# One pool open over the up and down stages of a hybrid layer: down's first operands split during up's last block, up's first sums on GpSimd

## Chip, cores and metric

The kernel runs on one core of one Trainium2 chip. The metric is the device time of one execution in microseconds, the median of several. Engines are named as in the profile: PE (TensorE, matrix products), ACT (ScalarE), DVE (VectorE), POOL (GpSimd) and SP (SyncE, which here only issues transfers).

## What is computed

One layer of a streaming encoder trunk, for 2048 frames of a new stream and 64 frames of a running one: 2112 tokens of 1024 features.

```python
x = x + mix @ lp['w_out']
f = jax.nn.relu(_rms(x, lp['ln2']) @ lp['w_up'])
x = x + (f * f) @ lp['w_down']
```

`mix` comes from attention, a state-space branch and a short convolution, which the change doesn't touch. `w_up` is 1024 x 4096, `w_down` 4096 x 1024. All values are fp32. A product of two fp32 matrices is made of three products of halves: each operand is split into a high part (ACT copies it to the type fp32r) and a low part (DVE subtracts that copy from the value), and the products high-high, high-low and low-high are summed.

## The kernel before

The program runs in stages: in-projection, attention with the other branches between it, the out-projection with the norm (`phase3a`), which leaves the normed tokens in DRAM as `h_d` and the new x as `x2_d`, then `phase_up` and `phase_down`. Every stage opens its own pools of tiles on chip and closes them. A tile scheduler decides at build time in which order each engine's instructions stand, from the order of the code, what is ready and which buffers are free; an instruction that is given to `keep_in_program_order` is not moved. Engines, and the queues that issue transfers, work in the order of their queue: an instruction that waits holds all behind it.

**phase_up** (line 1538) computes relu(h @ w_up) squared with Strassen's scheme, seven products of half blocks in place of eight (`ORDER`). Tokens come in 3 blocks of 704, in two halves of 352; the columns of `w_up` in 16 groups of 256. One group in one block is a pair, numbered n = 0 to 47; each has 7 products of 12 matmuls 128x352 (line 1630). For each token block four sums of halves are made (`sums`, lines 1569 to 1575, 128x1408) and seven splits (`tokens`, 1582 on ACT, 1583 on DVE); for each pair four weight sums (`weights`, 1593 to 1596) and seven weight splits (1600, 1601, 128x512). The sums stand on DVE, but the weight sums of pair 0 on POOL. `pair` empties the product banks into the tile `sm` (copies on ACT at 1641, 1644, 1647, adds on DVE at 1650 to 1656), applies relu and square and stores `sm` to DRAM as `f_d` from SP's queue. `late_rows` finishes the norm of the last 128 prompt rows meanwhile, out of buffers of the first block (`late_x` reuses the slot of `hr0`).

**phase_down** (line 1696) multiplies `f_d` by `w_down` in 8 quarters of 4 weight rows `dw` (128x1024 each, split at 1712 and 1713) and 17 token tiles, 24 matmuls 128x512 for each tile (lines 106 to 108), summed into `acc` by DVE at 1764. Tokens are loaded again from `f_d` (`fr`, line 1718, SP) and split into `fh` and `fl` (1733, 1734). In the very first tile the loop runs over weight rows outside and halves inside. Before that loop the code stands as

```python
    for f in range(QF):
        load_w(f, nc.gpsimd)
    for f in range(2):
        split_w(f)
    load_f(*work[0])
    split_f(*work[0])
    for f in range(2, QF):
        split_w(f)
```

so that none of it can begin before the up stage's pools are free.

## Time and profile before

| | us |
|---|---|
| timed runs, median (lowest, highest) | 2822.74 (2819.06, 2823.24) |
| profiled execution, its time | 2809.31 |
| its span in the trace | 2807.6 |
| PE busy in the span | 2689.5 (96%) |
| DVE busy | 1692.3 (60%) |
| ACT busy | 1231.5 (44%) |
| POOL busy | 409.5 (15%) |

All rows are of the profiled execution, and their times count from the start of its span. A row of a timeline is one instruction, or several alike that follow each other: its start, its length (for several, from the first start to the last end), engine, line, operation, output<-input, count, and in brackets how long the engine stood idle before it and what ended that. A matmul's length is modelled and overlaps the next, so starts are compared there. A row of windows gives the busy time of each engine in a stretch and the granted clock of PE as a share of 2.4 GHz.

### The profile page before, as it was taken

To read this page: it belongs to the slowest core of one execution; us is meant where nothing else is said; L and a number is where in the kernel's file an instruction comes from. 1 tells how busy PE (TensorE), PEld (TensorE's weight loads), DVE (VectorE), ACT (ScalarE), POOL (GpSimd) and SP (SyncE) were. 2 spreads that over 40 slices of the span, in tenths; PEclk is the share of its full clock that TensorE was granted. 3 is DMA by queue.
4 is the path that set the end of the run, shared out by engine and by line. 5 is a ranking of instruction groups with operands and counts; after the bars stand their busy time and mean duration, and the time that the engine had idled before them with its cause. 6 is when DMAs were issued, how large, how long until landed. Compare 5 with 4: busy or idle time off the path is not lost.

```text
span 2807.6 us, 38902 instructions
## 1 busy us (share of the span) xinstructions
PE 2689.5 (96%) x14438; PEld 2335.1 (83%) x14438; DVE 1692.3 (60%) x3375; ACT 1231.5 (44%) x2383; POOL 409.5 (15%) x570
## 2 busy tenths in 40 slices
PE   7999998778899999999899999999989999999999
PEld 7999998755566776688789999999978888888887
DVE  7637468478465677577686686676644344434433
ACT  5424243156577678833265576675631111111110
POOL 2101105122662225422200000000000000000000
PEclk9999999889899999999999999999999999999999
DMA  7535545543634134375535353343354222212123
GB/s 217 187 109 184 161 111 170 109 98 92 102 97 111 44 93 116 102 217 163 183 132 176 130 180 128 127 167 127 127 188 128 64 79 80 78 47 78 49 75 120
DMA packets 365712, 347.12 MB, mean 124 GB/s; under 512 B 43342, under 2 KB 324254, under 8 KB 362542
## 3 DMA queue, kind: packets, MB, share of 16 engines
q1 hardware_dynamic: 362707, 335.53, 41.2%
q0 software_dynamic: 2816, 9.11, 1.0%
q8 instruction: 114, 1.87, 0.3%
q14 instruction: 75, 0.61, 0.1%
HBM read 237.05 MB, written 107.46 MB: 123 GB/s over the span
## 4 chain that ended last, share of the span: by engine, by line
PE 83%; DMA 5%; DVE 4%; ACT 3%; issue 2%; POOL 2%; SPq 1%; DVEq 0%; ACTq 0%; POOLq 0%
PE pa L1630 13%; PE pd L106 8%; PE pd L107 8%; PE pd L108 8%; PE pd L1630 6%; PE pb L1630 3%; PE pq L108 2%; PE pq L106 2%; PE pq L107 2%; PE mx L1146 2%; PE st L1237 2%; PE po L106 2%; PE st L1238 2%; PE po L1258 2%; PE po L107 2%
## 5 line engine op out<-in xcount | busy, mean ns | idle before, releaser
L1764 DVE TENSOR_TENSOR acc<-acc,pd 128x512 f32<-128x512 f32 x272 | 186.9, 687 | 420.8 <-PE pd L108 415.4
L106 PE MATMUL pd<-dw,fh 128*128 128x512 f32 x1024 | 399.4, 390 | 9.6 <-ACT dw L1712 9.6
L107 PE MATMUL pd<-dw,fh 128*128 128x512 f32 x1024 | 399.5, 390 | 0.0
L108 PE MATMUL pd<-dw,fl 128*128 128x512 f32 x1024 | 399.3, 390 | 0.0
L1733 ACT ACTIVATE fh<-fr 128x512 fp32r<-128x512 f32 x128 | 81.0, 633 | 550.3 <-PE pd L107 541.1
L1250 DVE TENSOR_TENSOR pl<-p,ph 128x512 fp32r<-128x512 f32 (+2 forms) x242 | 179.1, 757 | 117.5 <-ACT ph L1249 107.4
L106 PEld LDWEIGHTS pd<-dw,fh 128*128 128x128 f32 x1024 | 192.8, 188 | 49.7 <-ACT dw L1712 9.9
L107 PEld LDWEIGHTS pd<-dw,fh 128*128 128x128 f32 x1024 | 192.9, 188 | 40.7 <-DVE dw L1713 0.8
L108 PEld LDWEIGHTS pd<-dw,fl 128*128 128x128 f32 x1024 | 192.8, 188 | 40.2
L1151 DVE TENSOR_REDUCE pm<-mx 128x1 f32<-128x512 f32 (+2 forms) x320 | 185.0, 606 | 60.0 <-PE mx L1146 36.0
L1246 ACT ACTIVATE p<-st 128x512 f32<-128x512 f32 (+2 forms) x320 | 165.8, 545 | 86.8 <-PE st L1242 42.9
L1630 PE MATMUL pa<-as,wt 128*128 128x352 f32 x1152 | 201.8, 323 | 0.0
L1630 PEld LDWEIGHTS pa<-as,wt 128*128 128x128 f32 x1152 | 187.6, 188 | 1.4 <-ACT sm L1647 0.7
L106 PE MATMUL pq<-wh,xh 128*128 128x384 f32 (+1 forms) x512 | 179.4, 350 | 5.1 <-ACT xh L233 4.7
L108 PE MATMUL pq<-wh,xl 128*128 128x384 f32 (+1 forms) x512 | 174.5, 341 | 0.6 <-DVE xl L234 0.3
L1249 ACT ACTIVATE ph<-p 128x512 fp32r<-128x512 f32 (+2 forms) x320 | 174.0, 581 | 2.1
L1601 DVE TENSOR_TENSOR wt<-tt,wt 128x512 fp32r<-128x512 f32 x192 | 131.6, 689 | 71.4 <-ACT wt L1600 68.1
L107 PE MATMUL pq<-wl,xh 128*128 128x384 f32 (+1 forms) x512 | 174.2, 340 | 0.0
L1601 DVE TENSOR_TENSOR w<-wr,w 128x512 fp32r<-128x512 f32 x144 | 99.1, 688 | 91.5 <-ACT w L1600 91.4
L1237 PE MATMUL st<-q,kb 67*128 67x512 f32 (+2 forms) x320 | 129.5, 406 | 22.1 <-DMA q<-m_d 12.3
L1600 ACT ACTIVATE wt<-tt 128x512 fp32r<-128x512 f32 x192 | 120.4, 628 | 67.2 <-PE pd L1630 66.1
L1600 ACT ACTIVATE w<-wr 128x512 fp32r<-128x512 f32 x144 | 90.3, 627 | 92.6 <-PE pa L1630 92.6
(489 smaller groups left out, 6105.2 us busy)
## 6 DMA issues: line engine op xcount, KB each, us to landing
wr<-in_w_up_dram SPq DMA_DIRECT2D x46, 1024.0 KB
f_d<-sm SPq DMA_DIRECT2D x48, 704.0 KB
fr<-f_d SPq DMA_DIRECT2D x128, 256.0 KB
raw<-in_w_in_dram SPq DMA_DIRECT2D x51, 512.0 KB
dr<-in_w_down_dram SPq DMA_DIRECT2D x28, 512.0 KB
qk_d<-stgT SPq DMA_DIRECT2D x16, 768.0 KB
xt<-in_x_prompt_dram SPq DMA_DIRECT2D x16, 512.0 KB
ka<-qk_d SPq DMA_DIRECT2D x16, 512.0 KB
```

Source lines behind the costliest of these rows:

```text
L106: nc.tensor.matmul(out, lh, rh, start=first, stop=False)
L107: nc.tensor.matmul(out, lh, rl, start=False, stop=False)
L108: nc.tensor.matmul(out, ll, rh, start=False, stop=last)
L1151: nc.vector.tensor_reduce(pm[:, t, c:c + 1], p[:, :n], axis=AX.X, op=ALU.max)
L1237: nc.tensor.matmul(st[:, c0:], kb[i][:, kc], q1[i][:, q0 + c0:q0 + 512], start=True, stop=False)
L1246: nc.scalar.activation(p[:, c0:], st[:, c0:], AF.Exp)
L1249: nc.scalar.activation(ph[:, c0:], p[:, c0:], AF.Copy)
L1250: (nc.gpsimd if g.idle and j else nc.vector).tensor_tensor(pl[:, c0:], p[:, c0:], f32(ph)[:, c0:], op=ALU.subtract)
L1600: ac.activation(t[:, 0], src[nm], AF.Copy)
L1601: ve.tensor_tensor(t[:, 1], src[nm], f32(t)[:, 0], op=ALU.subtract)
L1630: nc.tensor.matmul(bank, w[:, x, k], a[:, y, k], start=first and k + j == 0, stop=k + j == 5, skip_group_check=not first)
L1764: nc.vector.tensor_tensor(a[:, o], a[:, o], p, op=ALU.add)
```

## The change

A new pool `both` (`g.xp`) stays open over both stages. The token blocks `hr0`, `hr1` and the sums `st0` to `st2` of up live in it, and after them down's first operands.

- In up's first block, `sums(0)` is done by POOL; the loads of the weights of pairs 0 and 1 go out earlier on POOL's queue (the second no longer waits for a buffer); the token and weight splits of pair 0 alternate, one of each, and are pinned, as are the instructions that empty its banks.
- In up's last block, `down_start` goes one step further in each of eight pairs (f = 2 to 9): it loads `dw` rows 0 to 2 and the first token tile, and splits them, into the buffers of `hr0`, `hr1`, `st0` and `st1`, which that block no longer needs once its tokens are split.
- The store of the last pair is issued by ACT instead of SP.
- Down begins with the load and split of weight row 3 alone; its weight loads all stand on SP's queue.

```diff
+    xp = g.xp
-        hr[b] = [up.tile([128, 8, TH], F32, tag=f"hr{i}", name=f"hr{b}_{i}") for i in range(2)]
+        hr[b] = [xp.tile([128, 8, TH], F32, tag=f"hr{i}", name=f"hr{b}_{i}") for i in range(2)]
...
-        raw = raws[n] = up.tile([128, 8, 256], F32, tag="wr", bufs=2, name=f"wr{n}")
+        raw = raws[n] = up.tile([128, 8, 256], F32, tag=f"wr{n % 2}", name=f"wr{n}")
...
-        ve.tensor_tensor(s1, a21, a22, op=ALU.add)
+        eng = ve if b else po
+        eng.tensor_tensor(s1, a21, a22, op=ALU.add)
...
+    def split(t, x, pinned):
+        for i in (ac.activation(t[:, 0], x, AF.Copy),
+                  ve.tensor_tensor(t[:, 1], x, f32(t)[:, 0], op=ALU.subtract)):
+            if pinned:
+                tc.keep_in_program_order(i)
...
-        nc.sync.dma_start(g.f_d[256 * f:256 * f + 256, b * TB:b * TB + TB].rearrange("(e p) t -> p e t", p=128),
-                          sm.rearrange("p (e i) t -> p e (i t)", e=2))
-
-    load_h(0, nc.gpsimd)
+        eng = ac if n == 3 * (NF // 2) - 1 else nc.sync
+        eng.dma_start(g.f_d[256 * f:256 * f + 256, b * TB:b * TB + TB].rearrange("(e p) t -> p e t", p=128),
+                      sm.rearrange("p (e i) t -> p e (i t)", e=2))
+
+    def down_start():
+
+        for j in range(3):
+            r = xp.tile([128, D], F32, tag="st2", name=f"dr{j}")
+            nc.sync.dma_start(r, g.I["w_down"][0][j * 128:j * 128 + 128, :])
+            yield
+            if j < 2:
+                g.first[j] = xp.tile([128, 2816], F32R, tag=f"hr{j}", name=f"dw{j}")
+                hi, lo = g.first[j][:, 0:D], g.first[j][:, D:2 * D]
+            else:
+                hi, lo = (xp.tile([128, D], F32R, tag=f"st{i}", name=f"dw{j}_{i}") for i in range(2))
+            ac.activation(hi, r, AF.Copy)
+            ve.tensor_tensor(lo, r, f32(hi), op=ALU.subtract)
+            g.wts[j] = hi, lo
+            yield
+        r = xp.tile([128, 4, 128], F32, tag="st2", name="fr0_0")
+        nc.sync.dma_start(r, g.f_d[0:512, 0:128].rearrange("(f p) t -> p f t", p=128))
+        yield
...
+    load_h(0, po)
+    load_w(0, po)
     for _ in sums(0):
         pass
...
+    load_w(1, po)
+    start = zip(tokens(0), weights(0))
+    for _ in range(3):
+        next(start)
...
+            if b == 2 and 2 <= f < 10:
+                next(first, None)
...
-    for f in range(QF):
-        load_w(f, nc.gpsimd)
-    for f in range(2):
-        split_w(f)
-    load_f(*work[0])
-    split_f(*work[0])
-    for f in range(2, QF):
-        split_w(f)
+    load_w(3)
     load_f(*work[1])
+    load_x(0)
+    split_w(3)
     load_f(*work[2])
-    load_x(0)
     load_x(1)
```

The order of POOL's queue at the start of up, before (`hr` the token loads, `wr` the weight loads of pairs 0 and 1, `tt` the weight sums):

```order
L1555 DMA hr_0_15256<-h_d 128x4x352 x2
L1555 DMA hr_1_15257<-h_d 128x4x352 x2
L1561 DMA wr_15269<-in_w_up_dram 128x8x256
L1561 DMA wr_15318<-in_w_up_dram 128x8x256
L1593 TENSOR_TENSOR tt_15271<-wr_15269 128x512
L1595 TENSOR_TENSOR tt_15271<-wr_15269 128x512
L1594 TENSOR_TENSOR tt_15271<-wr_15269,tt_15271 128x512
L1596 TENSOR_TENSOR tt_15271<-wr_15269,tt_15271 128x512
```

and now (`s` the token sums):

```order
L1556 DMA hr_0_15259<-h_d 128x4x352 x2
L1556 DMA hr_1_15260<-h_d 128x4x352 x2
L1562 DMA wr_15265<-in_w_up_dram 128x8x256
L1572 TENSOR_TENSOR s_0_15267<-hr_1_15260 128x1408
L1562 DMA wr_15277<-in_w_up_dram 128x8x256
L1574 TENSOR_TENSOR s_0_15268<-s_0_15267,hr_0_15259 128x1408
L1578 TENSOR_TENSOR hr_1_15260<-hr_0_15259,hr_1_15260 128x1408
L1576 TENSOR_TENSOR s_0_15269<-hr_0_15259,s_0_15268 128x1408
L1601 TENSOR_TENSOR tt_15282<-wr_15265 128x512
L1603 TENSOR_TENSOR tt_15282<-wr_15265 128x512
L1602 TENSOR_TENSOR tt_15282<-wr_15265,tt_15282 128x512
L1604 TENSOR_TENSOR tt_15282<-wr_15265,tt_15282 128x512
```

Both weight loads went ahead of the arithmetic, and four token sums, the third of them in place in `hr1`, stand before the weight sums.

DVE's queue in the same place, before (`a`, `as` token splits; `s` and the row `hr<-hr,hr` token sums; `w`, `wt` weight splits):

```order
L1583 TENSOR_TENSOR a_0_15297<-hr_0_15256,a_0_15297 128x1408
L1583 TENSOR_TENSOR a_0_15312<-hr_0_15256,a_0_15312 128x1408
L1569 TENSOR_TENSOR s_0_15262<-hr_1_15257 128x1408
L1583 TENSOR_TENSOR a_0_15315<-hr_1_15257,a_0_15315 128x1408
L1571 TENSOR_TENSOR s_0_15263<-s_0_15262,hr_0_15256 128x1408
L1575 TENSOR_TENSOR hr_1_15257<-hr_0_15256,hr_1_15257 128x1408
L1573 TENSOR_TENSOR s_0_15264<-hr_0_15256,s_0_15263 128x1408
L1601 TENSOR_TENSOR w_0_15276<-wr_15269,w_0_15276 128x512
L1601 TENSOR_TENSOR wt_0_15279<-tt_15271,wt_0_15279 128x512
L1601 TENSOR_TENSOR wt_0_15282<-tt_15271,wt_0_15282 128x512
```

and now:

```order
L1583 TENSOR_TENSOR a_0_15279<-hr_0_15259,a_0_15279 128x1408
L1583 TENSOR_TENSOR w_0_15287<-wr_15265,w_0_15287 128x512
L1583 TENSOR_TENSOR as_0_15290<-s_0_15267,as_0_15290 128x1408
L1583 TENSOR_TENSOR wt_0_15293<-tt_15282,wt_0_15293 128x512
L1583 TENSOR_TENSOR as_0_15296<-s_0_15268,as_0_15296 128x1408
L1583 TENSOR_TENSOR wt_0_15299<-tt_15282,wt_0_15299 128x512
L1583 TENSOR_TENSOR as_0_15320<-s_0_15269,as_0_15320 128x1408
L1583 TENSOR_TENSOR w_0_15323<-wr_15265,w_0_15323 128x512
L1583 TENSOR_TENSOR as_0_15339<-hr_1_15260,as_0_15339 128x1408
L1583 TENSOR_TENSOR wt_0_15342<-tt_15282,wt_0_15342 128x512
```

The four token sums are gone from it, and each token split is followed by the weight split of the same product; ACT's copies stand in the same new order.

ACT's queue in the first pairs of up's last block as it is now (`sm` empties banks or applies relu, `a` and `as` token copies, `dw` down's weight row 0):

```order
L1582 ACTIVATE a_2_19464<-hr_0_18694 128x1408
L1582 ACTIVATE w_33_19495<-wr_19340 128x512
L1653 ACTIVATE sm_19519<-pa_19516 128x352
L1673 ACTIVATE sm_19371<-sm_19371 128x704
L1656 ACTIVATE sm_19519<-pd_19517 128x352
L1691 ACTIVATE dw_19998<-dr_19869 128x1024
L1582 ACTIVATE a_2_19480<-hr_1_18695 128x1408
L1671 ACTIVATE sm_19371<-pa_19368 128x352
L1674 ACTIVATE sm_19371<-sm_19371 128x352
```

The row `dw` is new, ahead of the block's last token copy; the others stood there before.

ACT's queue at the end of up, before:

```order
L1661 ACTIVATE sm_21388<-sm_21388 128x704
L1662 ACTIVATE sm_21388<-sm_21388 128x352
L1659 ACTIVATE sm_21388<-pa_21385 128x352
L1663 ACTIVATE sm_21388<-sm_21388 128x1408
L1733 ACTIVATE fh_0_21508<-fr_0_21506 128x512
L1733 ACTIVATE fh_1_21530<-fr_1_21518 128x512
L1712 ACTIVATE dw_21500<-dr_21492 128x1024
L1733 ACTIVATE fh_2_21566<-fr_2_21520 128x512
L1712 ACTIVATE dw_21503<-dr_21494 128x1024
L1712 ACTIVATE dw_21512<-dr_21496 128x1024
```

and now:

```order
L1673 ACTIVATE sm_21414<-sm_21414 128x704
L1674 ACTIVATE sm_21414<-sm_21414 128x352
L1671 ACTIVATE sm_21414<-pa_21411 128x352
L1675 ACTIVATE sm_21414<-sm_21414 128x1408
L1677 DMA f_d<-sm_21414 128x2x704
L1765 ACTIVATE dw_21524<-dr_21518 128x1024
L1786 ACTIVATE fh_1_21535<-fr_1_21520 128x512
```

One weight split and the store's issue are left between the last square and the token tile 1; three `dw` and the first `fh` have moved into the last block.

## Rows read from the trace of the kernel before

**Rows 1.** The page: one group of rows; busy, mean ns | idle before it, releaser

```profile
L106 PE MATMUL pd<-dw,fh 128*128 128x512 f32 x1024 | 399.4, 390 | 9.6 <-ACT dw L1712 9.6
```

**Rows 2.** Windows: length, PE, PEld, DVE, ACT, POOL busy, PEclk, DMA share, GB/s

```profile
1394.40:1406.10 11.70, 0.04 (x2) 0.02 (x1) 9.65 (x5) 6.45 (x7) 6.58 (x5) 0.68 0.60 180
1406.10:1416.30 10.20, 7.00 (x23) 6.17 (x24) 10.20 (x12) 8.94 (x13) 0.00 (x0) 0.53 0.28 74
1416.30:1441.80 25.50, 25.49 (x159) 25.09 (x158) 23.75 (x38) 14.74 (x29) 0.00 (x0) 1.00 0.49 164
2054.10:2065.70 11.60, 11.60 (x73) 11.31 (x71) 2.48 (x4) 2.68 (x5) 0.00 (x0) 1.00 0.16 62
...
2075.30:2081.00 5.70, 5.66 (x13) 3.97 (x14) 5.20 (x5) 3.29 (x4) 0.00 (x0) 0.50 1.06 367
```

**Rows 3.** Windows of line 1630 alone: length, PE, PEld busy, PEclk, DMA share, GB/s

```profile
1394.40:1441.85 47.45, 32.56 (x181) 31.34 (x182) 0.82 0.47 148
```

**Rows 4.** Timeline of DVE: start, us, line, operation, tiles, [idle before]

```profile
1301.33 3.17 DVE L1480 SCALAR_TENSOR_TENSOR hs<-x,oss,ln 128x1024 f32<-128x1024 f32 x1
...
1396.45 6.11 DVE L1583 TENSOR_TENSOR a<-hr,a 128x1408 fp32r<-128x1408 f32 x2 [2.12 <-ACT a L1582]
...
1410.76 1.28 DVE L1601 TENSOR_TENSOR wt<-tt,wt 128x512 fp32r<-128x512 f32 x2
...
1414.38 4.68 DVE L1583 TENSOR_TENSOR as<-s,as 128x1408 fp32r<-128x1408 f32 x3
...
1847.03 1.62 DVE L1583 TENSOR_TENSOR as<-s,as 128x1408 fp32r<-128x1408 f32 x1
...
2083.34 1.37 DVE L1764 TENSOR_TENSOR acc<-acc,pd 128x512 f32<-128x512 f32 x2 [2.85 <-PE pd L108]
```

**Rows 5.** Timeline of POOL

```profile
1301.00 2.40 POOL L1421 TENSOR_TENSOR mr<-mr 128x1024 f32<-128x1024 f32 x1 [5.70 <-ACT mr L1418]
1303.48 1.59 POOL L1422 TENSOR_TENSOR mr<-mr 128x256 f32<-128x256 f32 x1
...
1394.75 1.28 POOL L1593 TENSOR_TENSOR tt<-wr 128x512 f32<-128x512 f32 x1
...
1397.19 1.27 POOL L1594 TENSOR_TENSOR tt<-wr,tt 128x512 f32<-128x512 f32 x1
```

**Rows 6.** Chain that ended last, in order of time: start, us, what

```profile
2066.23 1.39 ACT sm L1663
...
2068.55 5.08 DMA fr<-f_d
...
2081.72 0.23 PE pd L108
```

**Rows 7.** Timeline of SP, whose rows issue the transfers

```profile
2054.11 13.88 SPq L1664 DMA_DIRECT2D f_d<-sm  x2
...
2076.55 0.51 SPq L1708 DMA_DIRECT2D dr<-in_w_down_dram  x1
...
2091.81 0.37 SPq L1708 DMA_DIRECT2D dr<-in_w_down_dram  x1
```

**Rows 8.** Instructions on the tiles hr, to 1440: duration ns min/median/max, first and last

```profile
L1555 POOL DMA_DIRECT2D hr<-h_d x4: 748/753/829, 1369.7 to 1372.0; - x4
...
DMA to landing us min/median/max: 6.2/9.0/10.9
```

**Rows 9.** Timeline of ACT

```profile
1853.02 1.39 ACT L1582 ACTIVATE a<-hr 128x1408 fp32r<-128x1408 f32 x1
...
1859.05 0.45 ACT L1647 ACTIVATE sm<-pa 128x352 f32<-128x352 f32 x1
...
2085.14 1.06 ACT L1712 ACTIVATE dw<-dr 128x1024 fp32r<-128x1024 f32 x1 [0.71 <-DMA dr<-in_w_down_dram]
...
2097.48 1.06 ACT L1712 ACTIVATE dw<-dr 128x1024 fp32r<-128x1024 f32 x1 [1.22 <-DMA dr<-in_w_down_dram]
```

**Rows 10.** Timeline of PE in the third block's first pairs

```profile
1859.91 2.08 PE L1630 MATMUL pa<-as,wt 128*128 128x352 f32 x12
```

More of the change, by code (lines that the diff above doesn't have):

```diff
@@ L1581, in tokens @@
             t = A[b, nm] = up.tile([128, 2, 4, TH], F32R, tag=f"a{i}", name=f"a{nm}_{b}")
-            ac.activation(t[:, 0], src[b][nm], AF.Copy)
-            ve.tensor_tensor(t[:, 1], src[b][nm], f32(t)[:, 0], op=ALU.subtract)
+            split(t, src[b][nm], b == 0)
             yield
@@ L1599, in weights @@
             t = up.tile([128, 2, 4, 128], F32R, tag="ws", bufs=10, name=f"w{nm}_{n}")
-            ac.activation(t[:, 0], src[nm], AF.Copy)
-            ve.tensor_tensor(t[:, 1], src[nm], f32(t)[:, 0], op=ALU.subtract)
+            split(t, src[nm], n == 0)
             wts[n, nm] = t
+            yield
     def late_rows():
-        xs = up.tile([128, 2, D], F32, tag="hr0", name="late_x")
-        ln = up.tile([128, D], F32, tag="st", bufs=3, name="late_ln")
+        xs = xp.tile([128, 2, D], F32, tag="hr0", name="late_x")
+        ln = xp.tile([128, D], F32, tag="st0", name="late_ln")
         x, hs = xs[:, 0, :], xs[:, 1, :]
@@ L1617, in late_rows @@
         yield
-        ht = up.tile([128, 8, 128], F32, tag="hr1", name="late_h")
+        ht = xp.tile([128, 8, 128], F32, tag="hr1", name="late_h")
         for j in range(2):
@@ L1663, in pair @@
         ac.activation(sm, sm, AF.Square)
-        nc.sync.dma_start(g.f_d[256 * f:256 * f + 256, b * TB:b * TB + TB].rearrange("(e p) t -> p e t", p=128),
-                          sm.rearrange("p (e i) t -> p e (i t)", e=2))
-    load_h(0, nc.gpsimd)
+        eng = ac if n == 3 * (NF // 2) - 1 else nc.sync
[17 more added lines that the diff above has]
+        nc.sync.dma_start(r, g.f_d[0:512, 0:128].rearrange("(f p) t -> p f t", p=128))
+        yield
+        h, l = (g.first[j][:, 2 * D:2 * D + 512].rearrange("p (f t) -> p f t", t=128) for j in range(2))
+        ac.activation(h, r, AF.Copy)
+        ve.tensor_tensor(l, r, f32(h), op=ALU.subtract)
+        g.fts[0, 0] = h, l
+    load_h(0, po)
+    load_w(0, po)
     for _ in sums(0):
         pass
-    load_w(0, nc.gpsimd)
-    weights(0)
-    for _ in tokens(0):
-        pass
-    load_w(1, nc.gpsimd)
+    for tag, shape, bufs in (("ws", [128, 2, 4, 128], 10), ("tt", [128, 4, 4, 128], 1), ("wr1", [128, 8, 256], 1)):
+        up.tile(shape, F32R if tag == "ws" else F32, tag=tag, bufs=bufs, name=f"{tag}_")
+    load_w(1, po)
+    start = zip(tokens(0), weights(0))
+    for _ in range(3):
+        next(start)
     late = late_rows()
     NP2 = NF // 2
-    nxt = iter(())
+    nxt, first = start, down_start()
     for b in range(3):
@@ L1684, in phase_up @@
                 load_h(b + 1)
-            if n + 1 < 3 * NP2:
-                weights(n + 1)
+            if 0 < n < 3 * NP2 - 1:
+                for _ in weights(n + 1):
+                    pass
             if b < 2 and f == NP2 - 3:
@@ L1691, in phase_up @@
             pair(b, f, lambda: next(nxt, None))
+            if n == 0:
+                for _ in weights(1):
+                    pass
             if b == 0 and f in (2, 4, 6):
                 next(late, None)
+            if b == 2 and 2 <= f < 10:
+                next(first, None)
 def phase_down(ctx, g):
@@ L1703, in phase_down @@
     QF = 4
-    raws, wts, fr, fts, acc = {}, {}, {}, {}, {}
+    raws, wts, fr, fts, acc = {}, g.wts, {}, g.fts, {}
     def load_w(f, eng=nc.sync):
@@ L1710, in split_w @@
     def split_w(f):
-        t = wts[f] = dp.tile([128, 2, D], F32R, tag=f"w{f % (2 * QF)}", name=f"dw{f}")
-        nc.scalar.activation(t[:, 0], raws[f], AF.Copy)
-        nc.vector.tensor_tensor(t[:, 1], raws[f], f32(t)[:, 0], op=ALU.subtract)
+        j = f % (2 * QF)
+        if j < 2:
+            t = g.xp.tile([128, 2816], F32R, tag=f"hr{j}", name=f"dw{f}")
+            hi, lo = t[:, 0:D], t[:, D:2 * D]
+        elif j == 2:
+            hi, lo = (g.xp.tile([128, D], F32R, tag=f"st{i}", name=f"dw{f}_{i}") for i in range(2))
+        else:
+            t = dp.tile([128, 2, D], F32R, tag=f"w{j}", name=f"dw{f}")
+            hi, lo = t[:, 0], t[:, 1]
+        wts[f] = hi, lo
+        nc.scalar.activation(hi, raws[f], AF.Copy)
+        nc.vector.tensor_tensor(lo, raws[f], f32(hi), op=ALU.subtract)
     def load_f(q, t):
@@ L1750, in products @@
             if t < 16:
-                mm3(nc, p, h[:, j], l[:, j], w[:, 0, o], w[:, 1, o], j == 0, j == QF - 1)
+                mm3(nc, p, h[:, j], l[:, j], w[0][:, o], w[1][:, o], j == 0, j == QF - 1)
             else:
-                mm2(nc, p, h[:, j], w[:, 0, o], w[:, 1, o], j == 0, j == QF - 1)
+                mm2(nc, p, h[:, j], w[0][:, o], w[1][:, o], j == 0, j == QF - 1)
         if q + t == 0:
@@ L1878, in hybrid_step_kernel @@
             phase3a(c3, g)
-    with ExitStack() as c4:
-        phase_up(c4, g)
-    with ExitStack() as c5:
-        phase_down(c5, g)
+    g.wts, g.fts, g.first = {}, {}, {}
+    with ExitStack() as c6:
+        g.xp = c6.enter_context(tc.tile_pool(name="both", bufs=1, reuse_waits="tile"))
+        with ExitStack() as c4:
+            phase_up(c4, g)
+        with ExitStack() as c5:
+            phase_down(c5, g)
     if dbg is not None:
```

26 lines of the change are left out of this document (15 added, 11 removed).

## The prediction

> **What bounds the kernel now.** I read the page first: the groups of TensorE rows with an idle time, and there the one place in the down stage where PE (TensorE) waits is 9.6 us before line 106, for ACT's weight split `dw` [rows 1]. Then the busy time by stretches around the two stage changes [rows 2]: PE stands almost still from 1394.40 to 1406.10 and again for the 9.6 us before 2075.30, and after each pause runs at a granted clock near 0.5 (10.2 us and 5.7 us long), which is the lower of its two levels, 1.2 GHz. Between the seams PE is full, so only what these two seams lose can be won, and whatever is put into the last up block can only cost.
>
> Seam one: in the 47.45 us after 1394.40, line 1630 issued about 180 matmuls [rows 3]. At full clock one takes 25.49 / 159 = 0.160 us [rows 2], so they are worth 29 us and 18.4 us are lost. The DVE timeline says to what [rows 4]: DVE (VectorE) comes to the first token splits at 1396.45, two of them take 6.11 instead of 2 x 1.56 because POOL (GpSimd) runs its weight sums then [rows 5], next stand the four token sums, of the same size, then weight splits (1.28 for two), then three more token splits (4.68 from 1414.38) and a last one, so that the splits end near 1420.6. DVE's queue feeds the first pair, not PE.
>
> Seam two is a chain with no slack [rows 6]: the last square (1.39) on ACT, pair 47's store, then the token load (5.08), which the SP queue issues only behind that store, since SP sat in it for 13.88 us [rows 7], then ACT's split, then matmuls at 0.43 us (5.66 us for 13) instead of 0.23. The first sum into `acc` starts at 2083.34 [rows 4].
>
> **Part 1, sums on POOL and splits in order.** Removed from DVE: four sums, 4 x 1.56 = 6.2 us. Added to POOL: the trace has no 1408-column sum there; a 1024-column one takes 2.40 [rows 5], so 3.30 scaled, and by the 1.28 of 512 columns 3.52. I take 3.30, the longer row being nearer. They start when the last token load has landed: issued by 1372.0, 10.9 us for the slowest [rows 8], so 1382.9. Four sums (13.2), the issue of wr1 (0.8, as the token loads') and one wait behind a DVE operation of phase3a (1.1) end at 1398.1; the four weight sums (5.1) follow. So 1.65 + 5.1 = 6.75 us of POOL's work is left when DVE starts its splits at 1396.45.
>
> This work costs DVE its full time. The row: 6.11 for two splits beside POOL; and at 1301 DVE's two-input operation took 3.17, ending 1.1 after POOL's 2.40 that had begun first, while POOL's next then took 1.59 behind it [rows 4, 5]. The Trainium skill ("SBUF — State Buffer", section "Who interferes with whom") calls the port pair that the two share an exclusive lock, and its summary of rules says to schedule "whichever is off the critical path"; this speaks against the change, which puts POOL's sums in front of a DVE that is on the path. The trace agrees about the blocking, and by that rule too the sum holds the 6.75.
>
> So DVE needs 7 x (1.56 + 0.64) = 15.4 us for the pinned pairs of splits and 6.75 of waiting: the last ends at 1396.45 + 22.15 = 1418.6. PE keeps up behind each split, at whichever clock, and does product 6 by 1420.5. Next on DVE: three adds and three weight sums of pair 1, 0.64 or less each, and its first split, to 1423.0 at the latest and 1422.0 if the adds, with a third fewer columns, are shorter by as much. From there pair 1 is bound by PE: 84 + 12 matmuls at 0.16 = 15.4 us, so the same 180 matmuls end between 1437.4 and 1438.5; I take 1438.1. Before, they end at 1441.84. **Gain 3.7 us.** In between stands one new order on ACT (ScalarE): line 1622, which reads late_x, comes ahead of pair 1's second weight split. Its load can go out only when hr0's last split is done (about 1415.4) and takes some 5.1, as the load of [rows 6], so until 1420.5; that split is needed after 1423, so pair 1's first product covers it, and without that cover it costs up to 2 us. Bounds: if POOL kept DVE out through its whole row of sums, the first splits would slip by about 4 us and the gain be -0.5 (rival A); if half of the 6.75 were not waited for, 3.7 + 3.4 = 7.1.
>
> **Part 2, down's first operands in the last up block.** Three weight loads, one token load, and their splits stand in SP, ACT and DVE in pairs 32 to 35. The split time itself (3 x 1.06 + 0.6 us on ACT) falls into its gaps. The new risk is a wait in an ordered queue: ACT's copy of dw0 waits for a load, and behind it stand the token copy a22 (1853.02 before) and all that feeds pair 33. dr0 goes into the slot of s4, free when DVE has split it (1847.03 + 1.62, so 1848.7) [rows 4]; ACT must begin the copy by about 1852.4 to be hardly late for a22, and has then almost no gap until the copy of 1859.05, whose bank the next pair's fifth product writes from 1859.91 on [rows 9, 10]. With landing time L the stall is therefore max(0, L - 3.75); counted in the same way, dw2 stalls from 5.5 and the tokens fr0_0 from 4.65; dw1 has time. DVE's half of the split waits behind ACT and delays pair 33's sums alike; this is the same stall, not a second one. What L is: 5.08 for the token load of the seam, 5.7 for a weight load of 512 KB (2091.81 to 2097.48, waited for), 8.6 under full DMA load (2076.55 to 2085.14) [rows 6, 7, 9]. The stalls are 1.8, 3.2 and 11.9 us in sum. I take the 5.08, with **-1.8 us**, since the DMA share here is nearer to the light 0.16 of a late up stretch than to the 1.06 at 2075 [rows 2]; range 0 to -3.2.
>
> **Part 3, the seam itself.** PE's first down matmul then needs nothing but a bank and operands split 200 us earlier, and starts at 2065.7 without a fall of the clock. Three weight rows carry 18 matmuls, 4.1 us, to 2069.8. The fourth, dw3, is loaded by SP behind pair 46's store, which is over by 2055 [rows 7]; even 8.6 us lands it by 2064. ACT splits it after the square (2066.23 + 1.39) and the issue of the store, now ACT's (0.5, as SP's in [rows 7]): 2068.1 + 1.06 = 2069.2, and DVE's half (two of a weight split's 0.64) until 2070.5. That is 0.3 to 0.8 us of stall. The first half's 21 matmuls then end at 2070.8 to 2071.3, and the first add, 2083.34 before, comes 12.0 to 12.5 us earlier. **Gain 12.3 us**, range 11 to 12.8. Late next: fr0_1 goes out before the store (with the last pair's fifth product, 24 matmuls or 3.9 us before 2065.7, so 2061.8 + 5.08 = 2066.9), and is split after dw3 by 2070 on ACT, needed at 2071.2; fr0_4 waits for the store and is needed four tiles of 24 x 0.23 us after 2065.7, at 2087.8. Moving the loads off POOL's queue costs nothing: nothing else stands in it after the weight sums.
>
> **Sum.** 3.7 - 1.8 + 12.3 = 14.2 us. The profiled run, 2809.3 with what lies around its span, becomes 2795.1; the timed median lies 13.4 above that run, so 2822.7 - 14.2 = **2808.5**.
>
> **Rivals.** *A, POOL keeps the port.* At 1397.19 POOL began its next sum though DVE had waited since 1396.45, and DVE's two splits came out only at 1402.56 [rows 4, 5]; against it speaks 1303.48, where POOL's next operation let DVE pass. If POOL's back-to-back token sums do so, DVE's norm of the last tile and the transposes behind it slip too: seam one -0.5, total 10.0, 2812.7. The skill's same section says that "issue order, not op shape, decides who blocks"; by that DVE would pass at each end of an instruction and my sum stands.
> *B, the loads of part 2 come late (slower).* ACT's in-order wait is 3L - 13.9 us in sum. The token loads of seam one took 6.2 to 10.9 [rows 8]. From L = 10.4 on, with seam one at -0.5, the stalls (17.4) pass the gain (11.8) by 5.6 us, and the kernel is slower; at 10.9 it is 18.8, so 2829.7. Against it: one load at a time there.
> *C, dw3 or fr0_1 wait for pair 47's store after all.* Then 2068.5 + 5.08 + 1.06 + 1.2 = 2075.8 is the end of dw3's split, 6 us of the 12.3 are lost: 2814.5.
> *D, the change doesn't do what it says:* the first down product still waits for a freed buffer or bank of the up stage, seam two stays, and 3.7 - 1.8 is left: 2820.8.
> *E, the lock costs half:* seam one 7.1, total 17.6, 2805.1.
>
> **How the numbers follow.** Forecast 0.62, A 0.14, E 0.06, C 0.08, D 0.06, B 0.04. The lower end is E with part 2 at nothing and seam two at 12.8 (19.9, so 2802.8) less 1.5 for the scatter of the runs, 2801; the upper is A with -3.2 and 11 (7.3, so 2815.4), plus 1.5, 2817. D, B and the ends of others lie outside. A change of 0.2%, 5.6 us, is about what a measurement of this kernel can tell from none. Forecast, A, E and C are faster by more (0.90, of which 0.02 is taken off for their tails), D with those is within, B slower.
>
> **What would show it.** In the trace of the changed kernel: the 9.6 us before line 106 gone, the clock at 1.0 from 2066 to 2081, the first add near 2071 when counted from the end of up. At seam one: POOL's sums about 3.3 us each from 1383, DVE's splits alternating with POOL's weight sums, PE's first matmul near 1397 to 1400, the last split at 1418. In pairs 32 to 35: ACT idle before `dw` and `fr0_0` for a load, with PE idle behind it of up to 3 us in all. I am wrong if PE's loss in the last block is above 3 us, if DVE gets to its first split only after 1400, or if the first down product still waits.

## The result, and the profile after

The changed kernel takes 2807.25 us (median of 4 runs, 2804.99 to 2809.03), the kernel before 2822.99 (4 runs, 2819.06 to 2824.25). The ratio is 0.9946 with a 95% interval of 0.9929 to 0.9963: 15.2 us faster, 10.4 to 20.0. (Ratios and their intervals are those on record; they are not the quotients of the medians beside them.) The forecast of 2808.5 us, 14.2 us faster, came true in total. Two of its three terms did not.

The two profiled executions can't be subtracted end from end. What runs ahead of seam one is the same code in both, but its last instruction, the last matmul of the out projection, starts 11.4 us later in the second:

```profile
1393.16 0.39 PE L108 MATMUL po<-wo_u,ml 128*128 128x512 f32 x1
```

```profile
1404.59 0.39 PE L108 MATMUL po<-wo_u,ml 128*128 128x512 f32 x1
...
1414.28 1.94 PE L1488 MATMUL pht<-ident,hs 128*128 128x128 f32 x8 [9.31 <-DVE hs L1480]
1418.69 0.66 PE L1638 MATMUL pa<-a,w 128*128 128x352 f32 x1 [2.47 <-ACT w L1582]
...
1437.31 0.58 PE L1638 MATMUL pd<-as,wt 128*128 128x352 f32 x2 [1.01 <-ACT wt L1582]
...
1453.28 2.09 PE L1638 MATMUL pd<-as,wt 128*128 128x352 f32 x12
```

The first fence is the PE timeline of the kernel before, the second that of the changed kernel. The row of 1453.28 follows 180 recorded matmuls of up; in the trace of before the same instruction starts at 1441.84, where the window of [rows 3] ends. I use it as a marker and read four stretches of each trace. Over all kernels of this study the last out-projection matmul starts anywhere from 1389.7 to 1406.7, whatever was changed behind it, so most of the scatter between executions lies ahead of the stretches. Up ends with these rows of 12 matmuls, of before and of the changed kernel; the last of the 12 starts at 2065.38 and at 2073.10.

```profile
2063.61 2.09 PE L1630 MATMUL pa<-a,wt 128*128 128x352 f32 x12
```

```profile
2071.33 2.10 PE L1638 MATMUL pa<-a,wt 128*128 128x352 f32 x12
```

| us | before | changed | forecast of the gain |
|---|---|---|---|
| seam one: last out-projection matmul to the marker | 48.68 | 48.69 | 3.7 |
| rest of up: marker to its last matmul | 623.5 | 619.8 | -1.8 (block 3) |
| seam two: up's last matmul to the first add into `acc` | 17.96 | 5.85 | 12.3 |
| first add to the end of the span | 724.3 | 724.3 | 0 |

**Seam one did not move.** The window of up's matmul line alone that answers to [rows 3], starting as far behind the last out-projection matmul, holds the same 181 matmuls in 47.50 us (47.45 before), at the same granted clock:

```profile
1405.80:1453.30 47.50, 32.81 (x181) 31.25 (x182) 0.82 0.38 126
```

What filled it is in the timelines of POOL, which answers to [rows 5], and of DVE, which answers to [rows 4]:

```profile
1394.43 3.24 POOL L1572 TENSOR_TENSOR s<-hr 128x1408 f32<-128x1408 f32 x1 [9.36 <-DMA hr<-h_d]
1397.61 0.90 POOL L1562 DMA_DIRECT2D wr<-in_w_up_dram  x1
1398.53 3.25 POOL L1574 TENSOR_TENSOR s<-s,hr 128x1408 f32<-128x1408 f32 x1
1401.73 3.23 POOL L1578 TENSOR_TENSOR hr<-hr,hr 128x1408 f32<-128x1408 f32 x1
1404.91 3.14 POOL L1576 TENSOR_TENSOR s<-hr,s 128x1408 f32<-128x1408 f32 x1
1408.02 1.25 POOL L1601 TENSOR_TENSOR tt<-wr 128x512 f32<-128x512 f32 x1
1409.24 1.25 POOL L1603 TENSOR_TENSOR tt<-wr 128x512 f32<-128x512 f32 x1
1410.46 1.25 POOL L1602 TENSOR_TENSOR tt<-wr,tt 128x512 f32<-128x512 f32 x1
1411.79 1.27 POOL L1604 TENSOR_TENSOR tt<-wr,tt 128x512 f32<-128x512 f32 x1
```

```profile
1397.71 0.16 DVE L128 TENSOR_TENSOR rm_h<-rm_h,rt_h 128x1 f32<-128x1 f32 x1
1397.91 0.16 DVE L129 TENSOR_SCALAR rm_h<-rm_h 128x1 f32<-128x1 f32 x1
1398.10 13.63 DVE L130 TENSOR_TENSOR oss<-rm_h,rt_h 128x1 f32<-128x1 f32 x1
...
1412.31 1.82 DVE L1480 SCALAR_TENSOR_TENSOR hs<-x,oss,ln 128x1024 f32<-128x1024 f32 x1
...
1418.15 1.63 DVE L1583 TENSOR_TENSOR a<-hr,a 128x1408 fp32r<-128x1408 f32 x1
```

Of the two weight loads only the first stands ahead of all arithmetic on POOL, otherwise than said above; the second is issued at 1397.61, behind the first sum. Read the third DVE row: an operation on 128x1 numbers, whose like at 1397.71 (two inputs as well, while POOL issued that load) took 0.16 us, took 13.63. It ended at 1411.73, in the only gap between two of POOL's sums there, the 0.08 us between 1411.71 and the row of 1411.79, whose instruction reads what the one just ahead of it wrote. Everything on DVE stood behind it: the norm of the last tile (1412.31), for which PE's transposes waited 9.31 us, and the first split, at 1418.15. From there DVE ran its 14 splits of pair 0 without a pause, at 1.62 and 0.68 us, and the last ended at 1433.20, 28.6 us after the last out-projection matmul. Before, it was about 27.4 (1420.6 from [rows 4], less 1393.16). The four sums that DVE was spared, and the better order of its splits, paid for a wait that was not there before.

**Seam two did what was forecast.** The group of [rows 1], with its 9.6 us before line 106, reads now

```profile
L106 PE MATMUL pd<-dw,fh 128*128 128x512 f32 x1016 | 395.2, 389 | 0.0
```

and the seam itself, by the timelines of SP, PE, ACT and DVE (ACTq is ACT's issue of the store), with the window that answers to the last of [rows 2]:

```profile
2062.28 0.42 SPq L1752 DMA_DIRECT2D dr<-in_w_down_dram  x1
...
2069.59 0.36 SPq L1771 DMA_DIRECT2D fr<-f_d  x1
...
2073.26 0.39 PE L106 MATMUL pd<-dw 128*128 128x512 f32 x1
...
2073.95 1.38 ACT L1675 ACTIVATE sm<-sm 128x1408 f32<-128x1408 f32 x1
...
2075.37 0.39 ACTq L1677 DMA_DIRECT2D f_d<-sm  x1
2075.81 1.06 ACT L1765 ACTIVATE dw<-dr 128x1024 fp32r<-128x1024 f32 x1 [0.47 <-ACT sm L1675]
2076.90 1.22 DVE L1766 TENSOR_TENSOR dw<-dr,dw 128x1024 fp32r<-128x1024 f32 x1 [3.67 <-ACT dw L1765]
...
2077.38 0.61 PE L106 MATMUL pd<-dw,dw 128*128 128x512 f32 x2
...
2078.18 0.50 PE L107 MATMUL pd<-dw,dw 128*128 128x512 f32 x1 [0.18 <-DVE dw L1766]
...
2078.95 0.69 DVE L1817 TENSOR_TENSOR acc<-acc,pd 128x512 f32<-128x512 f32 x1 [0.22 <-PE pd L108]
```

```profile
2072.90:2078.90 6.00, 5.82 (x27) 4.56 (x26) 2.16 (x3) 4.46 (x6) 0.00 (x0) 1.00 1.02 369
```

PE goes from up's last product (last matmul at 2073.10) to down's first at 2073.26, keeps the clock at 1.00 where it was 0.50, loses a fraction of a microsecond to `dw3`'s second half, and the first add comes 5.85 us after up's last matmul.

**Block 3 costs nothing that can be seen.** SP's issues of `dr0`, `dr2` and `fr0_0`, and ACT's copies of them:

```profile
1856.55 0.34 SPq L1684 DMA_DIRECT2D dr<-in_w_down_dram  x1
...
1889.35 0.34 SPq L1684 DMA_DIRECT2D dr<-in_w_down_dram  x1
...
1898.89 0.37 SPq L1696 DMA_DIRECT2D fr<-f_d  x1
```

```profile
1860.20 1.06 ACT L1691 ACTIVATE dw<-dr 128x1024 fp32r<-128x1024 f32 x1 [0.53 <-DMA dr<-in_w_down_dram]
...
1893.70 1.06 ACT L1691 ACTIVATE dw<-dr 128x1024 fp32r<-128x1024 f32 x1 [1.34 <-DMA dr<-in_w_down_dram]
...
1902.28 0.62 ACT L1699 ACTIVATE dw<-fr 128x512 fp32r<-128x512 f32 x1
```

From issue to copy it is 3.65, 4.35 and 3.39 us (a last copy that waits for nothing is an upper bound of the landing), all below the prediction's thresholds of 3.75, 5.5 and 4.65. ACT waits 0.53 and 1.34 us, and PE has no gap there.

So the stretches give 0 + 0 + 12.1 us. The rest of up is no term: it lies between 619.8 and 623.5 us in all kernels of the study, 621.5 in one without part 2 and 623.2 in one with it. It is the pace of the whole stretch that differs: its last quarter, in which PE waits for nothing, takes 155.89 us before and 154.96 in the changed kernel.

### The profile page after: what moved, and what is told of

Read it like the earlier page. It is cut to its first block, busy times and chain, and to the rows that moved or that the text cites. A ratio compares the mean times of both kernels' runs of the same rounds, so it can differ in the third digit from the quotient of the medians.

```text
span 2803.3 us, 38893 instructions
## 1 busy us (share of the span) xinstructions
PE 2694.8 (96%) x14438; PEld 2338.4 (83%) x14438; DVE 1689.9 (60%) x3371; ACT 1229.4 (44%) x2383; POOL 417.8 (15%) x570
## 4 chain that ended last, share of the span: by engine, by line
PE 87%; DMA 5%; DVE 3%; ACT 2%; issue 2%; SPq 1%; POOL 0%; ACTq 0%; DVEq 0%; POOLq 0%
PE pa L1638 13%; PE pd L107 8%; PE pd L108 8%; PE pd L106 8%; PE pd L1638 6%; PE pb L1638 3%; PE pq L108 3%; PE pq L106 3%; PE pq L107 3%; PE mx L1146 2%; PE po L106 2%; PE po L108 2%; PE po L107 2%; PE st L1238 2%; PE st L1237 2%; PE po L1258 2%
## 5 line engine op out<-in xcount | busy, mean ns | idle before, releaser
L106 PE MATMUL pd<-dw,fh 128*128 128x512 f32 x1016 | 395.2, 389 | 0.0
L107 PE MATMUL pd<-dw,fh 128*128 128x512 f32 x1016 | 395.2, 389 | 0.0
L1250 POOL TENSOR_TENSOR pl<-p,ph 128x512 fp32r<-128x512 f32 (+1 forms) x78 | 94.7, 1216 | 248.6 <-ACT ph L1249 177.6
```

The lines of the kernel that those rows point to most:

```text
L106: nc.tensor.matmul(out, lh, rh, start=first, stop=False)
L107: nc.tensor.matmul(out, lh, rl, start=False, stop=False)
L1250: (nc.gpsimd if g.idle and j else nc.vector).tensor_tensor(pl[:, c0:], p[:, c0:], f32(ph)[:, c0:], op=ALU.subtract)
```

## The experiments

The theory after the result: only seam two pays; seam one is eaten by POOL, which keeps the port that it shares with DVE, and so holds DVE off, for as long as its instructions follow each other without a gap. The rival: part 1 does save the few microseconds forecast, and something else in the seam (a load, the order of the splits, `late_x`) takes them back. Each expectation counts seam one up to the 181st recorded matmul, taken within a group of rows; that point stands 0.3 to 0.7 us ahead of the marker in every kernel, so differences between kernels are what to compare. "Seam one" and "seam two" below are the stretches of the table above. Kernels that share a median of before ran on the same chip.

**Each seam alone.** Without part 1 (pair 0's loads, sums and order as before; the pool, the loads in block 3 and seam two as changed):

```diff
-        eng = ve if b else po
+        eng = ve
...
-            split(t, src[b][nm], b == 0)
+            split(t, src[b][nm], False)
...
-    load_w(1, po)
-    start = zip(tokens(0), weights(0))
```

> The changed kernel with its first part undone: in up's first block the sums are on DVE, the splits unpinned, the weight loads where they were; the operands of down are still split early. Theory P (POOL kept the port all through its sums, so the first part gave nothing): as fast as the changed kernel, about 12 us under before (ratio 0.9957). Theory F (the forecast's terms): 3.7 us slower than the changed kernel, since the first part is worth that. In the trace: from the last matmul of line 108 in the out-projection to the 181st of up 48.7 us, as before and as in the changed kernel; the first add into acc 12 us nearer to the end of up than before.

Measured: 2798.44 us against 2813.52, ratio 0.9954 (0.9940 to 0.9968), 12.9 us faster (9.0 to 16.9). Seam one 47.45, seam two 5.85. And part 1 alone, with down's start and the last store as before:

```diff
-        eng = ac if n == 3 * (NF // 2) - 1 else nc.sync
...
-            if b == 2 and 2 <= f < 10:
-                next(first, None)
...
-    load_w(3)
+    for f in range(QF):
+        load_w(f, nc.gpsimd)
```

> The first part alone: sums on POOL, pinned splits, earlier weight loads; nothing of down is loaded or split in up's last block, and the last store is SP's again. Theory P: no faster than before, ratio 1.000, DVE's small two-input operation of the last norm waits some 13 us behind POOL's sums, and the stretch from the last out-projection matmul to up's 181st is 48.7 us as before. Theory F: 3.7 us faster, 0.9987, stretch 45.

Measured: 2812.80 against 2813.52, ratio 0.9991 (0.9979 to 1.0004). Seam one 48.24, seam two 18.21; DVE's line 130 waits as in the whole change:

```profile
1395.87 13.62 DVE L130 TENSOR_TENSOR oss<-rm_h,rt_h 128x1 f32<-128x1 f32 x1
```

By the times alone either theory could stand: the first interval holds 12 us as well as the 10.5 that are left of the forecast's 14.2 without part 1's 3.7, the second 1.000 as well as 0.9987. The stretches decide, since theory F puts seam one near 45 us where part 1 is in. The gain is seam two's, alone and together. In the five traces of this study that have part 1 just as changed, seam one takes 48.2 to 48.7 us; in the two without it 47.45 and 48.68. Part 1 is worth nothing, to within about 1 us.

**POOL's sums as a chain.** The same sums on POOL, but ordered and pinned so that nearly each reads what the one just ahead wrote (s1, s2, s4, then s3; t1, t2, t4, then t3), with the second weight load ahead of them:

```diff
-        eng.tensor_tensor(s1, a21, a22, op=ALU.add)
+        pin = tc.keep_in_program_order if b == 0 else lambda i: i
+        pin(eng.tensor_tensor(s1, a21, a22, op=ALU.add))
...
+        if n == 0:
+            pin(eng.tensor_tensor(t4, b21, t2, op=ALU.subtract))
+        pin(eng.tensor_tensor(t3, b22, b12, op=ALU.subtract))
...
-    for _ in sums(0):
-        pass
...
+    for _ in sums(0):
+        pass
```

> The changed kernel with POOL's eight sums pinned in the order s1, s2, s4, s3, t1, t2, t4, t3, so that s2, s4, t2 and t4 each read what the instruction just ahead wrote. Theory P1 (DVE gets the port only where POOL's next instruction has to wait for the one ahead, which leaves a gap of about 0.08 us between them): DVE's operation of the last norm waits for one sum, 3.3 us at most, the norm's product is ready some 10 us earlier, the first split starts near 4 us after the last out-projection matmul instead of 13.6, and the stretch to up's 181st matmul falls from 48.7 to about 46. Theory P2 (POOL keeps the port as long as it has anything in its queue): the wait stays at 13 us, the stretch at 48.7.

Measured: seam one 43.41, 5.3 us shorter than in the changed kernel, twice what theory P1 expected; seam two 5.84. Time 2799.00 against 2813.52, ratio 0.9946 (0.9929 to 0.9963). The timelines of DVE and POOL:

```profile
1397.09 0.15 DVE L129 TENSOR_SCALAR rm_h<-rm_h 128x1 f32<-128x1 f32 x1
1397.28 2.90 DVE L130 TENSOR_TENSOR oss<-rm_h,rt_h 128x1 f32<-128x1 f32 x1
...
1400.76 3.79 DVE L1480 SCALAR_TENSOR_TENSOR hs<-x,oss,ln 128x1024 f32<-128x1024 f32 x1
...
1408.35 1.96 DVE L1584 TENSOR_TENSOR a<-hr,a 128x1408 fp32r<-128x1408 f32 x1
```

```profile
1396.92 3.23 POOL L1575 TENSOR_TENSOR s<-s,hr 128x1408 f32<-128x1408 f32 x1
1400.23 3.23 POOL L1577 TENSOR_TENSOR s<-hr,s 128x1408 f32<-128x1408 f32 x1
1403.42 4.17 POOL L1579 TENSOR_TENSOR hr<-hr,hr 128x1408 f32<-128x1408 f32 x1
...
1408.90 2.53 POOL L1604 TENSOR_TENSOR tt<-wr,tt 128x512 f32<-128x512 f32 x1
```

Line 130 now takes 2.90 us instead of 13.63: it waits for one sum, from 1396.92 to 1400.15, and gets in at the gap behind it (its end at 1400.18, the next sum's start at 1400.23). From then on the two engines alternate: POOL's sum at 1403.42 is lengthened to 4.17 by DVE's norm, its weight sum at 1408.90 to 2.53 by DVE's first split. The work is the same and in the same engines; only POOL's order was changed, the weight load's place in it with the sums'. Two kernels further below remove sums from POOL: with only s1 and s2 there, and the load still between them, line 130 takes 3.69 us, and with none it takes 0.16:

```profile
1395.10 0.16 DVE L130 TENSOR_TENSOR oss<-rm_h,rt_h 128x1 f32<-128x1 f32 x1
```

So it is POOL's sums that line 130 waits for, and how many of them it waits for goes by how many there are and in which order. This shows the cause. It doesn't show a rule for when DVE gets in: DVE passed also at 1403.46, where POOL's next sum follows without a gap and does not read the one ahead.

**Is it the loads of block 3?** `dr0` loaded twice over, the same bytes into the same place, so that it lands later and the stall of part 2 can be priced:

```diff
-            nc.sync.dma_start(r, g.I["w_down"][0][j * 128:j * 128 + 128, :])
+            for _ in range(2 if j == 0 else 1):
+                nc.sync.dma_start(r, g.I["w_down"][0][j * 128:j * 128 + 128, :])
```

> The changed kernel with down's weight row 0 loaded twice in a row into its buffer, so that ACT's copy waits for the second landing. In the changed kernel one load took 3.65 us from SP's issue to the start of ACT's copy and PE lost nothing. With two, 7.3 to 8 us. Theory S (the forecast's reckoning, stall = landing time - 3.75): PE stands 3.5 to 4.3 us in all in the first two pairs of the last block. Rival: the slack is larger than reckoned, and PE loses under 1 us.

Inconclusive. SP issued the pair at 1853.17, for 3.85 us, but the order of the instructions was planned anew and put ACT's copy at 1864.41, behind the token copy and the splits of pair 33, so that it waited for nothing. One execution took 2801.73 us, with seam one at 48.64, the rest of up 621.9. The price that the prediction set on a late load, ACT's wait in order, stays untested.

**DVE instead of POOL.** If POOL's lock is the loss, the sums can go back to DVE, each pinned just ahead of the split that needs it. With s1 and s2 on POOL and the rest on DVE:

```diff
+        pin(ve.tensor_tensor(s4, a12, s2, op=ALU.subtract))
...
+            if b == 0 and nm in ("s4", "s3"):
+                next(first_sums)
...
+            if n == 0 and nm in tsum:
+                tc.keep_in_program_order(ve.tensor_tensor(*tsum[nm], op=ALU.subtract))
```

> The changed kernel with only s1 and s2 of the first block on POOL; the other two token sums and pair 0's four weight sums stand on DVE, each pinned just ahead of the split that needs it. Theory P1 (POOL's row without gaps cost the first part its gain): with POOL free after s2, DVE's last norm is done within 2 us of the last out-projection matmul; DVE then has 15.4 us of splits and 5.6 of sums, to about 24.5, so up's 181st matmul comes at 43 to 44 us instead of 48.2, 4 to 5 us faster than the changed kernel, near 0.993 of before. Rival (the splits' own length sets the end, not the lock): 47 to 48.

Measured: seam one 51.45, 2.8 us longer than in the changed kernel; time 2808.09 against 2814.06, ratio 0.9975 (0.9960 to 0.9989). And with all of them on DVE (`po if b == 0 and False`, the splits of s2, s4 and s3 each behind their sum):

> The changed kernel with no arithmetic on POOL in up's first block: all four token sums and pair 0's weight sums on DVE, pinned just ahead of the split that needs each. If the order of need is what helps and POOL's help is paid back in waits, DVE needs 15.4 + 6.2 + 2.5 us from about 1 us after the last out-projection matmul, so 25, and the 181st matmul of up comes at 43.5 to 45, within 1.5 us of the variant with two sums on POOL. If POOL's sums are worth their time, it is 3 us later than that variant.

Measured: seam one 54.19; 2805.45 against 2814.06, ratio 0.9967 (0.9947 to 0.9987). Both fell far outside the 43 to 45 us that were expected; the second is 2.7 us behind the first, near the 3 that its rival gave, that POOL's sums are worth their time. Line 130 takes 3.69 and 0.16 us in them, so the loss is another. ACT and DVE of the first of the two:

```profile
1417.35 1.38 ACT L1585 ACTIVATE as<-s 128x1408 fp32r<-128x1408 f32 x1 [2.29 <-DVE s L1579]
```

```profile
1415.69 1.62 DVE L1579 TENSOR_TENSOR s<-hr,s 128x1408 f32<-128x1408 f32 x1
1418.76 1.62 DVE L1586 TENSOR_TENSOR as<-s,as 128x1408 fp32r<-128x1408 f32 x1 [1.44 <-ACT as L1585]
```

DVE makes the sum, ACT waits for it and copies it, DVE waits 1.44 us for that copy and only then subtracts. A sum that stands right ahead of its split makes the two engines take turns. If that is the reason, moving each sum one product ahead should win the loss back:

```diff
-            if b == 0 and nm in ("s4", "s3"):
+            if b == 0 and nm in ("s2", "s4"):
...
+            ahead = {"11": "t1", "t1": "t2", "22": "t3", "t3": "t4"}
+            if n == 0 and nm in ahead:
```

> The variant with only s1 and s2 on POOL, with every sum that DVE makes moved one product further ahead of its split. Just ahead of the split it cost 51.0 us to the 181st matmul, where 43 to 44 were expected; the traces show DVE waiting 0.7 to 1.4 us for ACT's copy after each sum, and ACT 2.3 us for each sum. If this ping-pong was the cause, 43 to 44 now; if DVE is simply too full without POOL, it stays near 50.

Measured: seam one 43.56, 7.9 us shorter than with the sums right ahead, and DVE has no such wait any more (ACT still waits 1.4 and 1.5 us for two of the token sums). Time 2795.72 against 2815.44, ratio 0.9928 (0.9908 to 0.9949).

**`late_x`.** The prediction saw that line 1622 now stands on ACT ahead of pair 1's second weight split, and took it as covered. In the trace after, ACT waits there for its load, and PE's gap of 1.01 us at 1437.31 is behind it:

```profile
1434.52 1.06 ACT L1622 ACTIVATE late_x<-late_x 128x1024 f32<-128x1024 f32 x1 [3.31 <-DMA late_x<-x_d]
```

With that one instruction pinned, so that it runs on ACT 88.5 us after the last out-projection matmul instead of 29.9, some four pairs later and not the two of the expectation:

```diff
-        ac.activation(hs, x, AF.Square, accum_out=ss)
+        tc.keep_in_program_order(ac.activation(hs, x, AF.Square, accum_out=ss))
```

> The changed kernel with the square of late_x on ACT pinned in its place in the code, two pairs later. In the changed kernel ACT stood 3.3 us before it for its load and PE 1.0 us behind that, in pair 1. If that wait is on the path, up's 181st matmul comes 1 to 1.5 us earlier (48.2 to about 47); if the splits on DVE hide it, nothing moves.

Measured: seam one 47.72, 1.0 us shorter than in the changed trace and 0.5 shorter than the shortest of the five with part 1 as changed, and PE's wait for ACT is gone (one execution, 2798.50 us; a single time can't tell 1 us, the stretch can).

**Who issues the last store?** Everything as changed, but pair 47's store back on SP, ahead of `dr3` and the token tiles:

```diff
-        eng = ac if n == 3 * (NF // 2) - 1 else nc.sync
+        eng = nc.sync
```

> The changed kernel with the store of the last pair issued by SP again, ahead of the loads of dw3 and the next token tiles. By the forecast's rival C the end of dw3's split moves by 6 us: from the last up matmul to the first add into acc 11.9 us instead of 5.85, and the kernel is about 6 us slower than the changed one, 0.9965 of before. If the store's place doesn't matter, 5.85 stays.

Measured: seam two 11.44, so 5.6 us of the 12.1 are lost, and 1.5 more behind it (first add to the end 725.8). Time 2811.24 against 2814.06, ratio 0.9992 (0.9971 to 1.0013); the 0.9965 that was expected lies just outside, and the stretches, with 6.5 us won at seam two and 1.5 lost behind it, come to 5 us or 0.9982. SP, ACT and DVE:

```profile
2066.86 13.89 SPq L1677 DMA_DIRECT2D f_d<-sm  x2
2080.84 0.42 SPq L1752 DMA_DIRECT2D dr<-in_w_down_dram  x1
```

```profile
2085.94 1.06 ACT L1765 ACTIVATE dw<-dr 128x1024 fp32r<-128x1024 f32 x1 [5.57 <-DMA dr<-in_w_down_dram]
```

```profile
2089.57 0.69 DVE L1817 TENSOR_TENSOR acc<-acc,pd 128x512 f32<-128x512 f32 x1 [0.71 <-PE pd L108]
```

The wait of SP in its queue that [rows 7] showed, 13.88 us, comes back as 13.89, `dr3` goes out behind it, and ACT waits 5.57 us. This is the prediction's rival C, built: it was priced at 6, which by its own end of `dw3`'s split (2075.8 against 2070.5) is 5.3.

**The changed kernel again, and two that join what paid.** On one chip, with the third of the DVE kernels above: the changed kernel as it is;

> The changed kernel itself, beside the three variants below and before on the same chip. By the stretches of the traces (0 at the first seam, 0 in the last block, 12.2 at the second) it should be 12 us faster than before, 0.9957; the forecast's 14.2 would be 0.9950.

the chain together with the pinned line 1622 (both diffs above);

> POOL's sums as the chain in which s2, s4, t2 and t4 read what stands just ahead, and the square of late_x pinned two pairs later. The chain alone brought up's 181st matmul from 48.2 to 42.8 us after the last out-projection matmul, the pinned square alone to 47.1. If the two add, 41.7, and the kernel is 6.5 us faster than the changed one and 18.7 faster than before (0.9934); if the square was in the chain's shadow, 42.8 and 5.4.

and this with the weight sums of pair 0 on DVE, one product ahead, and the four token sums as a chain on POOL:

```diff
-        eng = po if n == 0 else ve
...
+            ahead = {"11": "t1", "t1": "t2", "22": "t3", "t3": "t4"}
+            if n == 0 and nm in ahead:
+                tc.keep_in_program_order(ve.tensor_tensor(*tsum[ahead[nm]], op=ALU.subtract))
```

> The chain and the pinned square, with pair 0's weight sums on DVE, each one product ahead of its split, so that POOL is done with its token sums. In the chain variant DVE lost 3.6 us in its first four splits to POOL's weight sums; on DVE they cost 4 x 0.60 = 2.4 us. Expected 1 us earlier than with the weight sums on POOL: 40.7 to 41.7 us to the 181st matmul. If the lock costs less than the sums themselves, it is later.

| | median us | ratio to before (2815.44) | seam one | seam two |
|---|---|---|---|---|
| changed | 2803.11 | 0.9946 (0.9926 to 0.9965) | 48.43 | 5.84 |
| chain, line 1622 pinned | 2798.58 | 0.9942 (0.9925 to 0.9959) | 42.05 | 5.85 |
| two sums on POOL, the rest one product ahead on DVE | 2795.72 | 0.9928 (0.9908 to 0.9949) | 43.56 | 5.85 |
| chain, 1622 pinned, weight sums on DVE | 2797.74 | 0.9939 (0.9918 to 0.9960) | 40.98 | 5.84 |

The first row's interval holds both the 0.9957 of the stretches and the forecast's 0.9950. The chain (5.3) and the pinned line (1.0) add up to the 6.4 us of the second row. The last has the shortest seam one of all, 7.5 us below the changed kernel's beside it and 1.1 below the second row's, as expected. All three have lower medians than the changed kernel, by 4.5 to 7.4 us, but the intervals of the ratios overlap: by the stretches they are better, by the times alone that isn't settled.

## Why the prediction was right and wrong

**Seam two, right.** Shifted by the 7.56 us between 2065.70, where the prediction let down begin, and 2073.26, its steps are: `dw3`'s copy on ACT forecast at 2075.66, measured 2075.81; DVE's half done by 2078.1, measured 2078.12; a stall of 0.3 to 0.8, measured 0.34 (the row after the two matmuls of 2077.38 was due at 2077.84 by the pace of 0.23 and started at 2078.18); the first add 12.0 to 12.5 us earlier, measured 12.1. The clock stays at 1.00, as forecast. Rival C failed because ACT issues the store; the run with the store on SP shows that this line is worth 5.6 us of the seam. Rival D, a freed buffer or bank that is still waited for, failed: 0.16 us lie between the two stages' matmuls.

**Block 3, the term mis-sized.** The mechanism was stated as max(0, L - threshold), with L the landing time. L was taken as 5.08, from a load in the seam [rows 6] that ran at a DMA share of 1.08; the three loads here ran at 0.44, 0.64 and 0.66 and were in use after 3.65, 4.35 and 3.39. By the prediction's own formula that is 0 instead of 1.8, inside its bounds (0 to -3.2). Its reason, that the share here is nearer to 0.16 than to 1.06, holds for the first of the three alone, and as far as it held it spoke for a value below 5.08. Rival B falls with it. Whether PE would lose what the formula says stays open, since no run had a load later than its thresholds.

**Seam one, the step that failed.** The sum let DVE pass at every end of a POOL instruction, so that only 6.75 us of POOL's work would be waited for; the changed trace has DVE waiting from 1398.10 to 1411.7 through six sums, since POOL gave the port away only at its one gap. By the prediction's own sign, a first split only after 1400, this part was wrong: it came at 1418.15, which is 1406.72 with the shift of 11.43 us taken off. The Trainium skill ("SBUF — State Buffer", section "SBUF: two separate sides") says that whichever starts first, a VectorE operation with two SBUF inputs or a GpSimd operation that reads SBUF, gets the shared port pair for the whole instruction. Its section "Who interferes with whom" says that "issue order, not op shape, decides who blocks". The chained kernel agrees with the first: each side is held for one instruction of the other. The changed kernel does not agree with the second: line 130 has its start at 1398.10, while POOL issued a load, and the sum s2 at 1398.53, and yet line 130 came after s2 and after five more (starts on POOL are rough in a trace, but five instructions are not).

What stood around that step was sized well. POOL's sums were forecast to begin at 1382.9, in before's times; they began at 1394.43, so at 1383.0 with the shift taken off, and took 3.24 us each against 3.30. DVE's splits, 1.62 + 0.68 with about 0.08 of each overlapped, make 2.15 us for a pair of rows against 2.20. Two sums of the prediction are off by a little: its terms put the end of POOL's token sums at 1398.0, not 1398.1, and the early end of pair 1's first split at 1422.4, not 1422.0. Neither moves the 3.7 by more than 0.1.

Rival A was this mechanism, with a first split about 4 us late. It was 10.3 us late (1406.72 against 1396.45), because the norm of the last tile and its residuals stood behind the lock too; but the splits then ran free of POOL, and A's net of -0.5 for the seam was nearly what came, 0. With block 3 at nothing, A gives 11.8 us, and the stretches give 12.1. That the forecast's 14.2 came as near to the timed 15.2 is luck: its errors, 3.7 and -1.8, offset each other in part, and the interval of 10.4 to 20.0 can't tell 12 from 14. Its chance for A, 0.14, was too low: [rows 5] held one case for each behaviour, and the one at 1303.48, which spoke against A, had a gap of 0.08 us ahead of it, while the one at 1397.19, which spoke for it, had none. That difference stood in the trace (the sum ahead of 1397.19 starts at 1395.97 and takes 1.27) and was not used.

**`late_x`,** taken as covered, cost PE 1.0 us in the changed trace, within the 2 us that the prediction set if the cover was gone. The cover went because the splits slipped, and with them the end of `hr0`'s use, on which the load waits: its last split was forecast to be done at 1415.4 and was done at about 1430.4, so 1419.0 in before's times. The load went out at 1430.60 and was in use at 1434.52, so at 1423.1, where the forecast had it landed by 1420.5.

## What to carry to other kernels

Work that is moved to GpSimd beside a busy VectorE is costed by its gaps, not by its sum: a row of independent instructions there can hold a two-input VectorE operation off through all of it (13.63 us here), and an order in which nearly each reads the one ahead let the two alternate (2.90). A sum on VectorE that ScalarE must copy before VectorE can go on belongs one product ahead of its split. Where two executions differ ahead of the change by as much as the change is worth, compare from one common instruction to another.
